# A depthwise convolution computed in long rows on VectorE, started one weight block sooner, with the mean pooling in a lane of its own

## The chip, the cores and the metric

The kernel runs on one core of a Trainium2 chip. The metric is device time in microseconds (us) of one execution of the whole program; of several executions the median is taken. The engines are TensorE (PE in the profile, with its weight loads as PEld), VectorE (DVE), ScalarE (ACT), GpSimd (POOL) and SyncE (SP), which issues nearly all the DMAs here.

## The reference, cut to what matters

The reference is one step of a two-layer diffusion backbone: 128 prompt tokens and 2048 latent tokens of width 1024. Each layer projects the tokens once, cuts the 3072 result columns among four mixers of width 256, concatenates what they give (each gated by a SiLU) and projects again. The change touches two of the mixers, the pooling and the convolution:

```python
def trunk_layer(x, cond, p, ctx=None):
    h = x * (1 + scale) + shift
    u = h @ p['w_in'] + p['b_in']
    (a_x, a_g, nq, nk, nv, n_g, c_v, c_glu, c_g, gq, gk, gv, g_g) = jnp.split(u, SPLIT_POINTS, axis=-1)
    a_out = pool_mix(a_x, p['pool_w'], p['pool_scale'])     # centred means over 2, 4, 8, 16 tokens, minus self
    c_out = conv_mix(c_v, c_glu, p['conv_w'], p['conv_b'], p['conv_ln_g'], p['conv_ln_b'], p['conv_pw'])
    ...                                                     # neighbourhood attention, grouped-query attention
    mixed = jnp.concatenate([a_out * jax.nn.silu(a_g), n_out * jax.nn.silu(n_g),
                             c_out * jax.nn.silu(c_g), g_out * jax.nn.silu(g_g)], axis=-1)
    x = layer_norm(DEEPNORM_ALPHA * x + gate * (mixed @ p['w_out'] + p['b_out']), p['ln_g'], p['ln_b'])

def conv_mix(val, glu, w_dw, b_dw, g, b, w_pw):
    z = val * jax.nn.sigmoid(glu)
    z = lax.conv_general_dilated(z, ...) + b_dw             # 31 taps along the tokens, each channel by itself
    z = jax.nn.silu(layer_norm(z, g, b))                    # over the 256 channels
    return z @ w_pw
```

## The kernel before, in words

Each layer has four phases: phase 1 is the input projection and all that can be done beside it, phase 2 the grouped-query attention, phase 3 the neighbourhood attention, phase 4 the output projection with its LayerNorm. Only phase 1 is touched.

Phase 1 walks the tokens in two halves: three chunks of 384 tokens, then chunks of 384, 384 and 256 (`CH`, `HALVES`). In each half it goes through the twelve entries of `BLOCKS`, 256 result columns each: `cx0` and `cx1` (value and gate of the convolution, 128 channels each), `cg` (its output gate), `gkv` and `gq` (keys, values and queries of the grouped-query attention), `ax` and `ag` (pooling input and gate), `nv`, `nk`, `nq`, `ng`, `gg`. Each product is made of three passes over pairs of a high and a low part, since PE's fast format keeps fewer bits: L306 to L308. `prep_w` loads the next block's weights in two pieces and splits each: ScalarE writes the high part `whi` (L430), POOL subtracts it to get `wlo` (L431). In the first half the split weights are also stored, in the second they are loaded back.

A projection tile goes to a PSUM bank of a pool of five (`ps_u`). Tiles of `gkv`, `gq` and `nv` have tokens on the partitions and are emptied by VectorE (`evac_tok`, for `nv` into the tile `nve`, which a DMA then stores); the others have channels there and are emptied by ScalarE (`evac_ch`). For `gkv` and `gq` a key norm follows: a square on ScalarE (`sq`, L665), a sum on VectorE (`rs`, L668), a product and a split on POOL (`ks`, L729), transposes on PE into `ps_d` (L735). `ps_d` is a second pool, of three banks, which all the side work shares.

After every projection tile `tick()` runs. It takes pending steps of `Later` and then advances the lanes, which are lists of generators; each `yield` ends a step. Lane A has the convolution pieces (`conv_job`), lane B what follows each (`conv_post`) and the pooling pieces (`pool_job`), lane C the max passes of the neighbourhood attention, lane D the modulation. A piece (`CONV_JOBS`) is the prompt with 128 tokens or 252 latent tokens in the first half, 208 in the second; there are five in a half. `conv_job` loads a piece with its margins into `cz`, for both channel blocks of 128. VectorE does 22 of the 31 taps as multiply-adds into `cacc` (the first as a product); ScalarE does the other nine, each as a product (L767) that POOL adds to a second sum (L768), and POOL joins both sums (L776). Two pieces may be open at once, and their taps alternate. `conv_post` transposes a piece on PE, normalises it (L800 to L811), transposes it back, applies SiLU, splits it and multiplies by the pointwise weights. `pool_job` forms the window sums by doubling (L855 to L863), subtracts and scales, splits, multiplies by the group weights and gates.

The order that each engine follows is not the order of this code: a scheduler places the instructions by a simulated timeline when the kernel is built, with the order of emission and the `issue_after` marks as bounds. Each engine then works strictly in its order.

Of the kernel before, what the change touches and what calls it, by code (L numbers as in the profile page):

```python
# [39 lines left out]
]  # L40
BLOCKS = [
# [79 lines left out]
class Kern:  # L121
# [314 lines left out]
    def split(self, pool, tag, src_ap, shape, load_engine=None):  # L436

        nc = self.nc
        w = self.b1.tile(shape, F32, tag="j32", name="spl")
# [7 lines left out]
    def _phase1(self, l):  # L447
        nc, A, S, v = self.nc, self.A, self.S, self.lv[l]
        self.later = Later()
        laneA, laneB, laneC, laneD = Lane(), Lane(), Lane(), Lane()  # L450
        self.conv_open = 0
        self.cg_done = -1
# [22 lines left out]
        NA, NB = (1,1), (1,2)  # L475

        def tick(ins):

            self.later.tick()
            last.append(getattr(ins, "ins", ins))  # L480
            with self.tc.issue_after(last[-2] if len(last) > 1 else last[-1]):
                for _ in range(NA[half]):
                    laneA.step()
                for _ in range(NB[half]):
                    laneB.step()
                laneC.step()
                if len(last) % 2:
                    laneC.step()
                laneD.step()
# [3 lines left out]
        for half in range(2):  # L493
            for b, (name, _) in enumerate(BLOCKS):
# [54 lines left out]
        while laneA.step() | laneB.step() | laneC.step() | laneD.step():  # L549
# [126 lines left out]
    def rms(self, l, name, t0, nt, nh, qb, rs):  # L676
# [22 lines left out]
        def s2(t):  # L699
# [15 lines left out]
            if name == "gq":  # L715
# [6 lines left out]
                if tg == 0:  # L722
                    qp = self.rp.tile([128, 4, 2, 64], F32R, tag="qp", name="qp", bufs=1)
# [20 lines left out]
    def conv_job(self, l, job, laneB):  # L744
        nc, S, v = self.nc, self.S, self.lv[l]
        prompt, a, b, sz = job
        n = b - a
        while self.conv_open == 2:
            yield
        self.conv_open += 1  # L750
        z = self.b2.tile([128, 2, 286], F32, tag="cz", name="cz")
        src = S["z_p"] if prompt else S["z_l"]
        nc.sync.dma_start(z[:, :, :n + 30], src[:, a:b + 30].rearrange("(c p) t -> p c t", p=128))
        acc = self.b2.tile([128, 2, 256], F32, tag="cacc", name="cacc")
        yield
        i = 0
        for c in range(2):
            ac2 = self.b1.tile([128, 256], F32, tag="cac2", name="cac2")
            cw = v["cw"]
            nc.scalar.activation(  # L760
                ac2[:, :n], z[:, c, 0:n], AF.Identity, bias=v["cvec"][:, 0, c:c + 1], scale=cw[:, c, 0:1]
            )
            nc.vector.tensor_scalar(acc[:, c, :n], z[:, c, 1:1 + n], cw[:, c, 1:2], None, op0=ALU.mult)
            for k in range(2, CW):
                if k % 7 in (0, 3):
                    tm = self.b2.tile([128, 256], F32, tag="jo", name="ctm")
                    nc.scalar.activation(tm[:, :n], z[:, c, k:k + n], AF.Copy, scale=cw[:, c, k:k + 1])  # L767
                    nc.gpsimd.tensor_tensor(ac2[:, :n], ac2[:, :n], tm[:, :n], op=ALU.add)  # L768
                else:
                    nc.vector.scalar_tensor_tensor(  # L770
                        acc[:, c, :n], z[:, c, k:k + n], cw[:, c, k:k + 1], acc[:, c, :n], op0=ALU.mult, op1=ALU.add
                    )
                i += 1
                if i % 8 == 0:
                    yield
            nc.gpsimd.tensor_tensor(acc[:, c, :n], acc[:, c, :n], ac2[:, :n], op=ALU.add)  # L776
# [929 lines left out]
```

## Time and profile before

| | us |
|---|---|
| three executions | 2950.91, 2958.63, 2963.24; median 2958.63 |
| the profiled execution: its time | 2961.56 |
| its span (first to last instruction) | 2959.8 |
| busy in it: PE | 2780.4 (94%) |
| VectorE | 2010.5 (68%) |
| POOL | 1339.0 (45%) |
| ScalarE | 1221.3 (41%) |

The whole profile is one execution. Rows of the view by windows give, for a stretch of time, each engine's busy time with its instructions, PE's granted clock (1.00 is 2.4 GHz, 0.50 is 1.2 GHz) and the share of DMA in use. The list of waits names an engine's tile and line, then what released it. A timeline is the instructions of one engine in order of time; "x45" there means 45 of them in one row, and the time beside it is their sum. Shares of busy time over a whole span say little here, since phase 1 and the attention phases have different limits.

### The profile page before, as it was taken

The page shows a single profiled execution, that of the slowest core. Times are in us where ns is not written, and L with a number is a line of the kernel's source. Part 1 is how long each engine was busy: PE and PEld are TensorE (multiplying, and loading weights), DVE is VectorE, ACT ScalarE, POOL GpSimd, SP SyncE. Part 2 cuts the span into 40 slices and gives each one's busy share as a digit, 9 for nine tenths or more (in the row PEclk, how much of TensorE's full clock was granted, in tenths as well). Part 3 has the DMA queues.
Part 4 walks back from the last instruction along what each step waited for, and adds up shares of the span by engine and source line. Part 5 has one row for each costly group of instructions (what it writes and reads, how often), then busy time and mean ns, then how long its engine had stood idle before and what let it go on. Part 6 is the DMA issues. An engine that isn't in the chain of part 4 may idle for free. (4 is left out here: it accounts for less than half of the span.)

```text
span 2959.8 us, 46887 instructions
## 1 busy us (share of the span) xinstructions
PE 2780.4 (94%) x16944; PEld 2285.5 (77%) x16944; DVE 2010.5 (68%) x4119; ACT 1221.3 (41%) x2278; POOL 1339.0 (45%) x1074
## 2 busy tenths in 40 slices
PE   7988999999899999999989789989999999999998
PEld 6878999889655556887779789988995555578887
DVE  2696157965578886749854881579655888776587
ACT  4454433543344445542223554335423444465211
POOL 3676323542466666014326674245424666730232
PEclk9999999999999999999999999999999999999999
DMA  9655586566271005646754556744654511066442
GB/s 304 213 182 179 184 249 201 169 202 175 66 170 32 25 20 151 162 137 229 234 171 136 168 171 185 218 147 148 208 152 94 131 34 29 15 184 181 133 167 104
DMA packets 387464, 448.32 MB, mean 151 GB/s; under 512 B 53920, under 2 KB 342688, under 8 KB 385440
## 3 DMA queue, kind: packets, MB, share of 16 engines
q1 hardware_dynamic: 387232, 445.32, 49.9%
q8 instruction: 134, 2.20, 0.3%
q14 instruction: 98, 0.80, 0.1%
HBM read 279.82 MB, written 165.39 MB: 150 GB/s over the span
## 5 line engine op out<-in xcount | busy, mean ns | idle before, releaser
L306 PE MATMUL ps_u<-hhi,whi 128*128 128x384 f32 (+1 forms) x1728 | 572.2, 334 | 6.7 <-ACT hhi L389 6.7
L307 PE MATMUL ps_u<-hlo,whi 128*128 128x384 f32 (+1 forms) x1728 | 573.2, 332 | 1.8 <-POOL hlo L391 1.3
L308 PE MATMUL ps_u<-hhi,wlo 128*128 128x384 f32 (+1 forms) x1728 | 571.9, 331 | 0.7 <-POOL wlo L431 0.7
L1038 POOL TENSOR_TENSOR zp<-zp,e 128x1024 f32<-128x1024 f32 x160 | 386.6, 2416 | 206.4 <-ACT e L1020 202.9
L1020 ACT ACTIVATE e<-ps_d 128x1024 f32<-128x1024 f32 x288 | 292.1, 1025 | 358.3 <-PE ps_d L1015 342.6
L770 DVE SCALAR_TENSOR_TENSOR cacc<-cz,small,cacc 128x208 f32<-128x208 f32 (+2 forms) x840 | 402.8, 536 | 0.3
L306 PEld LDWEIGHTS ps_u<-hhi,whi 128*128 128x128 f32 x1728 | 329.2, 191 | 14.8 <-ACT hhi L389 9.3
L307 PEld LDWEIGHTS ps_u<-hlo,whi 128*128 128x128 f32 x1728 | 330.1, 191 | 5.6 <-POOL hlo L391 2.0
L308 PEld LDWEIGHTS ps_u<-hhi,wlo 128*128 128x128 f32 x1728 | 329.9, 191 | 1.9 <-POOL wlo L431 1.1
L768 POOL TENSOR_TENSOR cac<-cac,ctm 128x208 f32<-128x208 f32 (+2 forms) x320 | 235.8, 737 | 148.9 <-ACT ctm L767 103.9
L946 DVE TENSOR_REDUCE mx<-ps_s 128x1 f32<-128x512 f32 (+1 forms) x374 | 228.5, 631 | 104.3 <-PE ps_s L943 99.8
L1478 POOL TENSOR_TENSOR mlo<-mx,mhi 128x512 fp32r<-128x512 f32 x66 | 109.4, 1677 | 418.9 <-ACT mhi L1474 418.9
L1026 PE MATMUL ps_a<-e,gvv 128*64 128x512 f32 x1152 | 278.2, 604 | 0.0
L306 PE MATMUL ps_u<-whi,hhi 128*128 128x256 f32 x816 | 240.7, 295 | 4.0 <-ACT ev L558 4.0
L307 PE MATMUL ps_u<-wlo,hhi 128*128 128x256 f32 x816 | 237.4, 291 | 0.3 <-POOL wlo L431 0.3
L308 PE MATMUL ps_u<-whi,hlo 128*128 128x256 f32 x816 | 237.4, 291 | 0.0
L767 ACT ACTIVATE ctm<-cz,small 128x208 f32<-128x208 f32 (+2 forms) x320 | 148.0, 473 | 157.3 <-POOL cac L768 101.0
L431 POOL TENSOR_TENSOR wlo<-ws,whi 128x512 fp32r<-128x512 f32 x92 | 150.1, 1642 | 132.9 <-ACT whi L430 121.1
L1508 PE MATMUL ps_d<-wol,mhi 128*128 128x512 f32 x512 | 200.5, 392 | 0.0
L1507 PE MATMUL ps_d<-woh,mhi 128*128 128x512 f32 x512 | 200.4, 391 | 0.0
L1509 PE MATMUL ps_d<-woh,mlo 128*128 128x512 f32 x512 | 200.3, 391 | 0.0
L1015 PE MATMUL ps_d<-q,k 65*128 65x512 f32 x576 | 185.0, 402 | 13.0 <-DMA k<-s_k 13.0
(269 smaller groups left out, 5742.6 us busy)
## 6 DMA issues: line engine op xcount, KB each, us to landing
ws<-in_w_in SPq DMA_DIRECT2D x80, 256.0 KB
mw<-in_w_mod SPq DMA_DIRECT2D x32, 512.0 KB
nq<-s_nq SPq DMA_DIRECT2D x64, 256.0 KB
mx<-s_mix SPq DMA_DIRECT2D x16, 1024.0 KB
s_gate<-ev SPq DMA_DIRECT2D x80, 192.0 KB
s_qh<-qT SPq DMA_DIRECT2D x34, 256.0 KB
x<-in_x SPq DMA_DIRECT2D x17, 512.0 KB
s_xT<-xo SPq DMA_DIRECT2D x17, 512.0 KB
```

The lines of the kernel that those rows point to most:

```text
L306: mm(p, ah, bh, start=(k == 0), stop=False)
L307: mm(p, ah, bl, start=False, stop=False)
L308: return mm(p, al, bh, start=False, stop=(k == 7))
L768: nc.gpsimd.tensor_tensor(ac2[:, :n], ac2[:, :n], tm[:, :n], op=ALU.add)
L770: nc.vector.scalar_tensor_tensor(acc[:, c, :n], z[:, c, k:k + n], cw[:, c, k:k + 1], acc[:, c, :n], op0=ALU.mult, op1=ALU.add)
L946: r = nc.vector.tensor_reduce(mx[:, h, i:i + 1], p[:, :n], axis=AX.X, op=ALU.max)
L1020: nc.scalar.activation(e, s, AF.Exp)
L1026: nc.tensor.matmul(acc[kv * 64:(kv + 1) * 64, :], vv[:, j, kv * 64:(kv + 1) * 64], e[:, kv * 512:(kv + 1) * 512], start=(j == 0), stop=(j ...
L1038: nc.gpsimd.tensor_tensor(zp, zp, e, op=ALU.add)
L1507: nc.tensor.matmul(o, hi[:, k, :], woh[:, k, ns], start=(k == 0), stop=False)
L1508: nc.tensor.matmul(o, hi[:, k, :], wol[:, k, ns], start=False, stop=False)
L1509: nc.tensor.matmul(o, lo[:, k, :], woh[:, k, ns], start=False, stop=(k == 7))
```

## The change

The convolution of a half is one job now, instead of five. For each channel block of 128 it loads the half's whole row (`CONV_LEAD` = 158 columns of prompt with margin and 1008 latent columns in the first half, 1040 columns in the second) into one buffer `cz`, and does all 31 taps on VectorE over that whole row, each adding into the same `cacc`. Channel block 0 begins after block `cx0`, channel block 1 after `cx1`; before, nothing began until `cx1` was done. When all rows are done the five pieces go to `conv_post`, as before, without three idle steps in it and with one buffer `s32` for each channel block.

The pooling has its own lane P and works on one channel block of one piece at a time, with its own buffers (`px`, `pg`, `phi`, `plo`) and the next load issued ahead. `tick` takes one step of lane A in `gkv` and `gq` and two elsewhere, two of lane B, and one or two in turn of lanes P and C. `nve` has one buffer where it had two, `qp` takes the tag of `qd`, and `split` the tag `czs`.

```diff
@@ _phase1
-        NA, NB = (1,1), (1,2)
...
             with self.tc.issue_after(last[-2] if len(last) > 1 else last[-1]):
-                for _ in range(NA[half]):
+                odd = len(last) % 2
+                for _ in range(1 if name in ("gkv", "gq") else 2):
                     laneA.step()
-                for _ in range(NB[half]):
+                for _ in range(2):
                     laneB.step()
-                laneC.step()
-                if len(last) % 2:
+                for _ in range(2 if odd else 1):
+                    laneP.step()
                     laneC.step()
                 laneD.step()
...
+                if name == "cx0":
+                    laneA.add(self.conv_job(l, half, laneB))
                 if name == "cx1":
-                    for job in CONV_JOBS[half]:
-                        laneA.add(self.conv_job(l, job, laneB))
+                    self.cx1_done = half
                 if name == "ag":
-                    for job in CONV_JOBS[half]:
-                        laneB.add(self.pool_job(l, job))
+                    laneP.add(self.pool_jobs(l, half))
@@ evac_tok
-            e = self.e2.tile([128, 256], F32, tag="nve", name="nve")
+            e = self.e2.tile([128, 256], F32, tag="nve", name="nve", bufs=1)
@@ conv_job
-        while self.conv_open == 2:
+        a, b = CONV_SPAN[half]
+        lead = CONV_LEAD if half == 0 else 0
+        n = lead + b - a
+        acc = self.b1.tile([128, 2, CONV_LEAD + 1008], F32, tag="cacc", name="cacc")
+        for c in range(2):
+            while c == 1 and self.cx1_done < half:
+                yield
+            cs = slice(c * 128, (c + 1) * 128)
+            z = self.b1.tile([128, CONV_LEAD + 1008 + CW - 1], F32, tag="cz", name="cz")
+            if lead:
+                nc.sync.dma_start(z[:, :lead], S["z_p"][cs, :])
+            nc.sync.dma_start(z[:, lead:n + CW - 1], S["z_l"][cs, a:b + CW - 1])
             yield
...
-            nc.vector.tensor_scalar(acc[:, c, :n], z[:, c, 1:1 + n], cw[:, c, 1:2], None, op0=ALU.mult)
-            for k in range(2, CW):
-                if k % 7 in (0, 3):
-                    tm = self.b2.tile([128, 256], F32, tag="jo", name="ctm")
-                    nc.scalar.activation(tm[:, :n], z[:, c, k:k + n], AF.Copy, scale=cw[:, c, k:k + 1])
-                    nc.gpsimd.tensor_tensor(ac2[:, :n], ac2[:, :n], tm[:, :n], op=ALU.add)
-                else:
-                    nc.vector.scalar_tensor_tensor(
-                        acc[:, c, :n], z[:, c, k:k + n], cw[:, c, k:k + 1], acc[:, c, :n], op0=ALU.mult, op1=ALU.add
-                    )
-                i += 1
-                if i % 8 == 0:
-                    yield
-            nc.gpsimd.tensor_tensor(acc[:, c, :n], acc[:, c, :n], ac2[:, :n], op=ALU.add)
-        laneB.add(self.conv_post(l, job, acc), soon=True)
+            for k in range(1, CW):
+                nc.vector.scalar_tensor_tensor(
+                    acc[:, c, :n], z[:, k:k + n], cw[:, c, k:k + 1], acc[:, c, :n], op0=ALU.mult, op1=ALU.add
+                )
+                yield
+        for i, job in enumerate(CONV_JOBS[half]):
+            o = 0 if job[0] else lead + job[1] - a
+            laneB.add(self.conv_post(l, job, acc[:, :, o:o + job[2] - job[1]]))
@@ pool_job -> pool_jobs
+        items = [(job, c) for job in CONV_JOBS[half] for c in range(2)]
+        nxt = load_x(*items[0])
         yield
+        for i, (job, c) in enumerate(items):
+            x = nxt
...
+            nc.scalar.activation(yhi[:, :n], y, AF.Copy)
+            nc.gpsimd.tensor_tensor(ylo[:, :n], y, f32(yhi[:, :n]), op=ALU.subtract)
+            if i + 1 < len(items):
+                nxt = load_x(*items[i + 1])
             yield
...
```

The three places below show the order on an engine, before and after. The first is VectorE in layer 0, first half, where the convolution starts. `cacc` rows are convolution taps, `ev` the gating of the convolution's input, `qb` and `gve` the emptying of `gkv`, `mo` the modulation. Before:

```order
L770 SCALAR_TENSOR_TENSOR cacc<-cz,small,cacc 128x128 x2
L576 SCALAR_TENSOR_TENSOR ev<-ev 128x384
L770 SCALAR_TENSOR_TENSOR cacc<-cz,small,cacc 128x252 x2
L770 SCALAR_TENSOR_TENSOR cacc<-cz,small,cacc 128x128 x2
L770 SCALAR_TENSOR_TENSOR cacc<-cz,small,cacc 128x252 x2
L770 SCALAR_TENSOR_TENSOR cacc<-cz,small,cacc 128x128 x2
```

And of the change:

```order
L577 SCALAR_TENSOR_TENSOR ev<-ev 128x384 x3
L763 TENSOR_SCALAR cacc<-cz,small 128x1166
L767 SCALAR_TENSOR_TENSOR cacc<-cz,small,cacc 128x1166 x2
L577 SCALAR_TENSOR_TENSOR ev<-ev 128x384
L767 SCALAR_TENSOR_TENSOR cacc<-cz,small,cacc 128x1166 x11
L359 TENSOR_TENSOR mo<-mo,ps_d 2x128
L767 SCALAR_TENSOR_TENSOR cacc<-cz,small,cacc 128x1166 x7
L655 TENSOR_TENSOR qb<-ps_u,btok 128x128
L658 TENSOR_TENSOR gve<-ps_u,btok 128x128
```

The alternating short taps of two pieces have become rows of 1166 columns that all add into one buffer.

The second place is POOL from the same point on: `wlo` is the weight split, `cac` and `cacc` the convolution's adds, `qb` and `ks` the key norm. Before:

```order
L431 TENSOR_TENSOR wlo<-ws,whi 128x512 x4
L768 TENSOR_TENSOR cac_940<-cac_940,ctm 128x128 x6
L431 TENSOR_TENSOR wlo<-ws,whi 128x512
L768 TENSOR_TENSOR cac_940<-cac_940,ctm 128x128 x2
L431 TENSOR_TENSOR wlo<-ws,whi 128x512 x3
L776 TENSOR_TENSOR cacc<-cacc,cac_940 128x128
```

And of the change:

```order
L433 TENSOR_TENSOR wlo<-ws,whi 128x512 x12
L694 TENSOR_TENSOR qb<-qb,qkn 128x128 x3
L730 TENSOR_TENSOR ks<-qb,ks 128x2x64 x3
L694 TENSOR_TENSOR qb<-qb,qkn 128x128 x3
L433 TENSOR_TENSOR wlo<-ws,whi 128x512 x2
```

The convolution's adds are gone from between the weight splits.

The third place is VectorE in block `nv` of layer 0's second half: `nve` empties a projection tile, `mx` is a max pass, `cst`, `cmv`, `crs` and `czs` the normalisation of a convolution piece, `jo` a gated output, `pA` and `pB` window sums of the pooling. Before:

```order
L644 TENSOR_TENSOR nve<-ps_u,btok 128x256
L946 TENSOR_REDUCE mx<-ps_d 128x1
L644 TENSOR_TENSOR nve<-ps_u,btok 128x256 x3
L800 BN_STATS cst<-ps_d 104x6 x2
L802 BN_AGGR cmv<-cst 104x2 x2
```

And of the change:

```order
L645 TENSOR_TENSOR nve<-ps_u,btok 128x256
L834 TENSOR_TENSOR jo<-ps_d,jg 128x208 x2
L899 SCALAR_TENSOR_TENSOR jo<-ps_d,small,pg 128x208
L952 TENSOR_REDUCE mx<-ps_d 128x1 x2
L863 TENSOR_TENSOR pA<-px 128x223
L645 TENSOR_TENSOR nve<-ps_u,btok 128x256
L866 TENSOR_TENSOR pB<-pA 64x221
```

Between two emptyings there is now work of three lanes, where there was that of one or two.

## Rows read from the trace of the kernel before

**Rows 1.** View by windows: A and B stretches, and two single blocks; columns first.

```profile
core 0: us, PE busy (x) PEld busy (x) DVE busy (x) ACT busy (x) POOL busy (x), PEclk, DMA share, GB/s
90.20:269.80 179.60, 154.53 (x1110) 145.31 (x1109) 144.67 (x348) 93.33 (x209) 131.76 (x139) 0.95 0.58 187
269.80:422.50 152.70, 145.93 (x1049) 141.23 (x1047) 53.79 (x136) 54.15 (x113) 51.19 (x51) 0.98 0.66 207
476.70:626.90 150.20, 141.23 (x1101) 131.97 (x1098) 135.53 (x375) 73.00 (x173) 74.65 (x101) 0.99 0.63 199
626.90:761.40 134.50, 131.81 (x889) 128.54 (x888) 62.20 (x140) 45.67 (x99) 40.40 (x57) 1.00 0.50 152
1555.50:1580.80 25.30, 25.30 (x146) 25.30 (x145) 10.20 (x26) 9.57 (x22) 9.55 (x12) 1.00 0.48 156
1580.80:1761.10 180.30, 149.25 (x966) 145.04 (x964) 133.10 (x325) 91.71 (x194) 130.06 (x131) 0.92 0.50 160
1761.10:1894.60 133.50, 132.77 (x853) 132.17 (x852) 50.87 (x123) 50.99 (x102) 51.22 (x52) 1.00 0.65 196
1923.20:1946.70 23.50, 23.50 (x154) 23.50 (x154) 11.17 (x29) 4.58 (x10) 1.41 (x2) 1.00 0.50 150
1946.70:2094.10 147.40, 133.44 (x936) 130.86 (x935) 131.55 (x352) 70.70 (x163) 77.87 (x101) 0.94 0.55 173
2094.10:2230.60 136.50, 133.35 (x889) 129.56 (x888) 68.89 (x161) 46.48 (x99) 40.47 (x57) 0.99 0.51 149
```

**Rows 2.** View by windows, VectorE's instructions that read `cz` alone, four A stretches.

```profile
90.20:269.80 179.60, 87.34 (x180) 0.95 0.58 187
476.70:626.90 150.20, 90.16 (x201) 0.99 0.63 199
1580.80:1761.10 180.30, 84.56 (x165) 0.92 0.50 160
1946.70:2094.10 147.40, 85.89 (x186) 0.94 0.55 173
```

**Rows 3.** Weight splits (ns min/median/max), then timelines of VectorE and POOL: start, us.

```profile
L431 POOL TENSOR_TENSOR wlo<-ws,whi x92: 1263/1297/14333, 48.8 to 1872.2; 128x512 fp32r<-128x512 f32 x92
1589.63 17.59 DVE L770 SCALAR_TENSOR_TENSOR cacc<-cz,small,cacc 128x252 f32<-128x252 f32 x45
1594.03 14.33 POOL L431 TENSOR_TENSOR wlo<-ws,whi 128x512 fp32r<-128x512 f32 x1 [3.18 <-ACT whi L430]
```

**Rows 4.** Waits from 1605 to 1652 us: us in total, times, longest us.

```profile
DVE rs L668 <- ACT sq L665: 23.8, 6, 16.5
ACT cac L760 <- POOL cacc L776: 15.3, 3, 14.4
PE ps_d L735 <- POOL ks L729: 9.0, 1, 9.0
```

**Rows 5.** Timeline of VectorE from 2846 us (phase 4): start, duration.

```profile
2846.28 1.21 DVE L1500 TENSOR_TENSOR y<-ps_d,gb 128x1024 f32<-128x1024 f32 x1
2847.53 1.23 DVE L1501 TENSOR_TENSOR y<-y,x 128x1024 f32<-128x1024 f32 x1
2850.35 1.28 DVE L1524 SCALAR_TENSOR_TENSOR y<-y,mv,lng 128x1024 f32<-128x1024 f32 x1
```

**Rows 6.** Timelines of POOL and VectorE from 1329 us (phase 4).

```profile
1329.21 3.52 POOL L1478 TENSOR_TENSOR mlo<-mx,mhi 128x512 fp32r<-128x512 f32 x2
1329.29 2.29 DVE L1493 SCALAR_TENSOR_TENSOR x<-x,gbo 128x1024 f32<-128x1024 f32 x1 [2.60 <-POOL gbo L1458]
1331.61 2.20 DVE L1501 TENSOR_TENSOR y<-y,x 128x1024 f32<-128x1024 f32 x1
```

**Rows 7.** View by windows, line L811 alone, first A stretch.

```profile
90.20:269.80 179.60, 3.16 (x5) 0.95 0.58 187
```

**Rows 8.** Timelines of SP's queue and of VectorE, a load and its reader.

```profile
403.05 0.39 SPq L851 DMA_DIRECT2D px<-s_axl  x1
412.16 0.44 DVE L860 TENSOR_TENSOR pA<-px 128x267 f32<-128x267 f32 x1 [3.12 <-DMA px<-s_axl]
```

More of the change, by code (lines that the diff above doesn't have):

```diff
@@ L40 @@
 ]
+CONV_SPAN = [(0, 1008), (1008, 2048)]
+CONV_LEAD = NPR + CW - 1
 BLOCKS = [
@@ L438, in split @@
         nc = self.nc
-        w = self.b1.tile(shape, F32, tag="j32", name="spl")
+        w = self.b1.tile(shape, F32, tag="czs", name="spl")
         nc.sync.dma_start(w, src_ap)
@@ L722, in s2 @@
                 if tg == 0:
-                    qp = self.rp.tile([128, 4, 2, 64], F32R, tag="qp", name="qp", bufs=1)
+                    qp = self.rp.tile([128, 4, 2, 64], F32R, tag="qd", name="qp")
                     nc.vector.tensor_copy(qp, f32(ql).unsqueeze(2).to_broadcast([128, 4, 2, 64]))
@@ L742, in rms, with conv_job @@
             self.later.add(1 + (t + 1) // 2, lambda t=t: s2(t))
[L744 removed]
+    def conv_job(self, l, half, laneB):
         nc, S, v = self.nc, self.S, self.lv[l]
[L746 to L777 removed]
@@ L793, in conv_post @@
         nc.sync.dma_start(gt[:, :, :n], S["gate"][512:768, g0:g0 + n].rearrange("(c p) t -> p c t", p=128))
-        for _ in range(3):
-            yield
         for i in range(nt):
@@ L804, in conv_post @@
                 yield
-        self.conv_open -= 1
         yield
@@ L814, in conv_post @@
         yield
-        s32 = self.b1.tile([128, 2, 256], F32, tag="j32", name="j32")
+        yield
         shi = self.b1.tile([128, 2, 256], F32R, tag="jhi", name="jhi")
@@ L818, in conv_post @@
         for c in range(2):
+            s32 = self.b1.tile([128, 256], F32, tag="j32", name="j32")
             pj = self.bank("d")
@@ L865, in pool_job @@
                 nc.vector.tensor_tensor(B1[:, 2:m - 1], A1[:, 1:m - 2], A1[:, 3:m], op=ALU.add)
-                yield
                 nc.vector.tensor_tensor(A1[:, 4:m - 3], B1[:, 2:m - 5], B1[:, 6:m - 1], op=ALU.add)
                 nc.vector.tensor_tensor(B1[h, 8:m - 7], A1[h, 4:m - 11], A1[h, 12:m - 3], op=ALU.add)
+            yield
+            tmp = self.b1.tile([128, 2, 8], F32, tag="ptmp", name="ptmp")
+            ends = [(e, t0 - a) for e, t0 in ((0, 0), (1, seq - 8)) if a <= t0 < b]
@@ L872, in pool_job @@
                 )
-                for e, t0 in ((0, 0), (1, seq - 8)):
-                    if a <= t0 < b:
-                        o = t0 - a
-                        tmp = self.b1.tile([128, 8], F32, tag="ptmp", name="ptmp")
-                        nc.vector.tensor_tensor(tmp[r, :], f[r, 8 + o:16 + o], self.pedge[r, c, e, :], op=ALU.mult)
-                        nc.vector.tensor_tensor(y[r, c, o:o + 8], tmp[r, :], x[r, c, 8 + o:16 + o], op=ALU.subtract)
-            yield
-        yhi = self.b1.tile([128, 2, 256], F32R, tag="jhi", name="jhi")
@@ L881, in pool_job @@
-        ylo = self.b1.tile([128, 2, 256], F32R, tag="jlo", name="jlo")
-        for c in range(2):
-            nc.scalar.activation(yhi[:, c, :n], y[:, c, :n], AF.Copy)
-            nc.gpsimd.tensor_tensor(ylo[:, c, :n], y[:, c, :n], f32(yhi[:, c, :n]), op=ALU.subtract)
-        yield
-        yield
-        for c in range(2):
+            for e, o in ends:
+                nc.vector.tensor_copy(x[:, 8 + o:16 + o], tmp[:, e, :])
+            y = x[:, 8:8 + n]
+            yhi = self.b1.tile([128, 256], F32R, tag="phi", name="phi")
@@ L888, in pool_job @@
+            ylo = self.b1.tile([128, 256], F32R, tag="plo", name="plo")
+            nc.scalar.activation(yhi[:, :n], y, AF.Copy)
+            nc.gpsimd.tensor_tensor(ylo[:, :n], y, f32(yhi[:, :n]), op=ALU.subtract)
+            if i + 1 < len(items):
+                nxt = load_x(*items[i + 1])
+            yield
+            yield
             pj = self.bank("d")
-            nc.tensor.matmul(pj[:, :n], self.plh[:, c, :], yhi[:, c, :n], start=True, stop=False)
-            nc.tensor.matmul(pj[:, :n], self.plh[:, c, :], ylo[:, c, :n], start=False, stop=False)
```

58 lines of the change are left out of this document (34 added, 24 removed).

## The prediction

> **What bounds the kernel now.** I read the busy shares first (PE 94% of the span), then the granted clock and busy time stretch by stretch, then PE's waits and what lay before them, and last the VectorE and POOL timelines. Only phase 1 is touched. For each layer and half I cut it into A (blocks cg, gkv, gq, ax, ag) and B (nv, nk, nq, ng, gg), at the first projection matmul of a block; [rows 1] gives these eight stretches.
>
> The floor is PE's. A block that nothing disturbs takes 25.3 us in the first half and 23.5 in the second, with PE busy throughout at clock 1.00, the full 2.4 GHz [rows 1]. That last one holds 10 other matmuls besides its 144. The price of such an "other" matmul (transposes, finishing products) comes from B of layer 1's first half: 133.5 us against 5 x 25.3 = 126.5, with 853 records of which 792 are projections, so 7.0 / 61 = 0.115 us each. A second-half block without them is then 23.5 - 1.1 = 22.4 us. PE's order holds 172 and 100 others in A of the first halves (layer 0, layer 1) and 199 and 117 in the second, so if nothing waited the four would need 146, 138, 135 and 126 us. They take 179.6, 180.3, 150.2 and 147.4 [rows 1]. So some 113 us are lost in A, and little in B.
>
> What is lost there is PE waiting on a coupled VectorE, ScalarE and POOL. VectorE is busy 144.7 of 179.6 us, and 87.3 of that is convolution [rows 1, 2]. The worst case can be read event by event: VectorE runs 45 convolution ops in one unbroken train, 17.6 us, 0.391 us apart; a POOL subtraction that splits weights, whose median is 1.30 us, starts inside the train and takes 14.33 us [rows 3]. POOL is in order, so its convolution add behind it is late; ScalarE's next convolution op waits 14.4 us for that add, the square for the key norm behind it on ScalarE is 16.5 us late to VectorE, and PE then stands 9.0 us for the split keys [rows 4]. The clock of that A stretch is 0.92 [rows 1]: part of it ran at the lower level, after PE had stood idle.
>
> **The change, part by part.** *Convolution off ScalarE and POOL.* 320 ScalarE products, 320 POOL adds and 40 joining adds go. All 31 taps are on VectorE now: 248 long rows (1166 columns in the first half, 1040 in the second) for 880 short ones. Nothing on ScalarE waits for POOL's convolution any more, so the chain of [rows 4] can't form.
>
> *What a long row costs.* Each row adds into the same accumulator as the one before it, and so waits for it. A dependent op starts 0.03 to 0.04 us after its forerunner ends: 2846.28 + 1.21, then 2847.53 [rows 5]. A multiply-add with a pointer scalar over 1024 columns takes 1.28 us [rows 5], so 1.31 per link. The slope is at most (1.28 - 0.391) / (1024 - 252) = 1.15 ns a column, hence 1.31 + 142 x 0.00115 = 1.47 us for 1166 columns and 1.33 for 1040. Lower bound: no gap and 1.04 ns (1.28 us less a start of 0.21, estimated): 1.42 and 1.30.
>
> *POOL against VectorE.* In the old train POOL stayed out. At a dependent boundary it gets in: the subtraction of 1329.21 takes its turn, the op of 1331.61 waits 0.03 us for its forerunner, and both VectorE ops stretch, to 2.29 and 2.20 us from the 1.23 of 2847.53 [rows 5, 6]. So one POOL op of 512 columns costs the VectorE chain up to 0.97 us. Averaged over all sizes the trace shows less: 172 convolution ops at 0.391 (132 of them) and an estimated 0.27 (40) make 62 us, and 87.3 with the 8 first taps (4 us) were busy, so 21 us over 139 POOL ops, 0.15 each [rows 1, 2]. In the order of the changed kernel A keeps 56 POOL ops in a first half (20 of them the weight splits) and about 33 in a second, where the split weights are reloaded. I take 0.97 for half of the 20 and 0.15 for the rest: 17 us; second half 33 x 0.15 = 5. Bounds: 56 x 0.15 = 8 and twice my value.
>
> The Trainium skill, SBUF — State Buffer, Who interferes with whom, says that a VectorE op with two SBUF inputs and a POOL op that reads SBUF exclude each other, and that the second to issue blocks until the first finishes. Under that rule the weight split would have waited for one op of 0.39 us, not 13 us; here the trace differs. The rule speaks against the change, as each block now lasts three times as long: an estimate by it is 56 x 1.0 = 56 us more POOL waiting per first half, which POOL, with 30 to 50 us of work left in 150, would still hide, so the sum would be the same.
>
> *A, summed.* VectorE's other work there is its busy time less the convolution [rows 1, 2], less about 9 us of finishing ops that move to B (an estimate: three times their largest member, 3.16 us, [rows 7]). By the order 62, 53, 54 and 54 of the long rows fall into A.
> - Layer 0, first half: 62 x 1.47 = 91, other 57.3 - 9 = 48, POOL 17: 156, and 5 for idle. PE needs 126.5 + 132 others x 0.115 = 142. So 161.
> - Layer 1, first half: 79 + 39.5 + 17 = 136 and 5; PE 133. So 141.
> - Layer 0, second half: 70.5 + 36 + 5 = 112; PE 112 + 134 x 0.115 = 127. So PE, 131 with some waits.
> - Layer 1, second half: 72 + 36.5 + 5 = 114; PE 118. So 122.
>
> That is 555 us for 657.5: -102.
>
> *B gets work.* Finishing (normalisation, pointwise product) and pooling of all five pieces of a half now follow in B, twelve steps each, two per tick, pooling in its own lane. By PE's order 243 more other matmuls stand in the four B stretches: x 0.115 = +28. The lag that nv carries in layer 0's first half (152.7 us, PE's need 126.5 + 157 x 0.115 = 144.6) mostly goes: -5. Chains with three PSUM banks between them will make PE wait a little; the second-half B of layer 1 shows 136.5 against 112 + 121 x 0.115 = 126, some 10 us over for three finished pieces and the wide max passes; for two pieces more I add 3.5 a half: +14. Bounds: 0 and +40.
>
> *At no cost.* The new `nve` single buffer, the merged `qp` tag, `czs` for the weight loads, the accumulator's single buffer: covered by PE running ahead over five banks, and by pieces being done before the next half's convolution starts; the first of these is priced as a rival.
>
> Sum: -102 + 28 - 5 + 14 = -65 us on the profiled execution of 2961.6: 2896. It lies 2.9 above the median of the runs, 2958.6, so about 2893; its span is 1.8 below its time.
>
> **Rivals.**
> 1. *Neither VectorE nor the chains ever bind.* Then A is PE's need, 142 + 133 + 127 + 118 = 520, -137; +28, -5: -114, 2845. For it: ScalarE and POOL are relieved. Against: in a first half VectorE is over PE's need even on the lower bounds (62 x 1.42 + 48 + 8 = 144).
> 2. *VectorE becomes the bound outright.* Twice the collisions in the first halves, 176 and 156, and 138 and 130 with waits behind rows of 1.4 us in the second: A 600, -57; +28 - 5 + 14: -20, 2939. For it: the token blocks gkv and gq are emptied by VectorE, now from behind long rows.
> 3. *Slower: the single `nve` buffer.* VectorE may not empty the next token tile of nv before the store of the last has landed, and max reductions, statistics and gated outputs wait behind it, with PE's three banks. PE delivers a tile about every 25.3 / 9 + 0.8 = 3.6 us. A transfer issued at 403.05 was waited for until 412.16, 8.7 us after its issue [rows 8]; with 0.42 for the op and 0.32 to issue that makes 9.4 us a tile, 5.8 too many, x 34 tiles = +197, less the 14 already counted: 3076. It decides from the point where it eats 79 us, 2.3 a tile, or a landing of 5.2 us; many transfers were quicker.
> 4. *POOL is starved by the long chain.* If dependence gives it no entry, the weight splits of gkv wait through the 18 rows in cg, 26 us, in both first halves, and PE behind them, partly at the lower clock: +26 to +52 and as much again in gkv: 2960 or so, no change. Against it: [rows 6]. This would also be the case in which the change doesn't loosen the coupling.
>
> **How the numbers follow.** Forecast 0.50, rival 1 0.15, rival 2 0.15, rival 3 0.12, rival 4 0.08. No change means within 0.5%, 15 us, about what a measurement of this kernel can tell. Forecast and rival 1 are faster but for 0.015; rival 2 sits on that edge, 0.09 faster and 0.06 same; rival 3 0.02 same and 0.10 slower; rival 4 0.02, 0.03, 0.03. That makes 0.75, 0.12, 0.13. The forecast's own range is 2870 to 2920. The range for 8 in 10 reaches down to rival 1 (2843) and up past rivals 2 and 4 to 2964; most of rival 3 stays outside.
>
> **What would show it.** Right: A of the first halves near 160 and 141 us with VectorE over 90% busy and PE's clock near 1; second halves at PE's pace; long rows 1.4 to 1.5 us apart, stretched by about 1 us where a weight split gets in; no POOL op beyond some 3 us in A; ScalarE never waiting for POOL there; B longer by 5 to 10 us each. Wrong: VectorE idle in A while PE waits (chains bind, not throughput); POOL ops of tens of us (rival 4); VectorE waiting for `s_nv` stores in nv (rival 3); or B longer by 20 us and more.

## The result and the profile after

The changed kernel takes 2887.55 us (median of 4 runs, 2885.37 to 2889.32) against 2959.32: a ratio of 0.9761, 95% interval 0.9739 to 0.9782. The forecast was 2893. Its profiled execution took 2889.32 us with a span of 2887.5, 72.3 shorter than before.

The view by windows, the same eight stretches as in [rows 1]: A, then B, of layer 0's first half and second half, then of layer 1's.

```profile
core 0: us, PE busy (x) PEld busy (x) DVE busy (x) ACT busy (x) POOL busy (x), PEclk, DMA share, GB/s
89.70:248.00 158.30, 147.59 (x1071) 139.20 (x1070) 151.90 (x239) 49.94 (x114) 75.77 (x57) 0.98 0.64 205
248.00:412.00 164.00, 155.34 (x1115) 147.03 (x1113) 53.67 (x136) 63.90 (x131) 51.62 (x53) 1.00 0.69 215
462.10:592.50 130.40, 129.59 (x1037) 122.81 (x1033) 111.58 (x206) 36.01 (x87) 39.13 (x33) 1.00 0.69 215
592.50:731.60 139.10, 137.24 (x946) 134.54 (x944) 62.04 (x155) 49.30 (x96) 25.03 (x33) 1.00 0.50 151
1543.90:1696.20 152.30, 139.23 (x927) 137.19 (x926) 141.85 (x222) 50.44 (x106) 67.32 (x57) 0.96 0.55 179
1696.20:1842.60 146.40, 142.69 (x920) 139.47 (x920) 52.36 (x123) 61.53 (x119) 50.49 (x52) 1.00 0.66 203
1892.90:2012.10 119.20, 118.14 (x871) 117.27 (x869) 112.25 (x196) 33.33 (x75) 36.00 (x33) 1.00 0.59 188
2012.10:2153.60 141.50, 137.40 (x946) 134.02 (x944) 62.80 (x157) 49.60 (x97) 24.82 (x33) 1.00 0.53 154
```

The four A stretches lost 97.3 us (560.2 for 657.5), the four B gained 33.8, the blocks `cx0` and `cx1` lost 7.7, all else 1.1. ScalarE's and POOL's busy time in A of the first halves has about halved (93 to 50, 132 to 76 us), VectorE's has grown. The same windows for the instructions that read `cz` answer to [rows 2]: VectorE spends more time on the convolution in a first half than before, less in a second.

```profile
89.70:248.00 158.30, 99.46 (x62) 0.98 0.64 205
462.10:592.50 130.40, 69.93 (x53) 1.00 0.69 215
1543.90:1696.20 152.30, 86.14 (x53) 0.96 0.55 179
1892.90:2012.10 119.20, 73.16 (x55) 1.00 0.59 188
```

The weight splits (ns: least, median, most), then VectorE and POOL in the place of [rows 3], answer to the shut-out there: the longest split is 2.64 us instead of 14.33. A row alone takes 1.42 us; beside a split it takes 2.26.

```profile
L433 POOL TENSOR_TENSOR wlo<-ws,whi x92: 1274/1308/2639, 49.5 to 1823.5; 128x512 fp32r<-128x512 f32 x92
```

```profile
1576.56 1.42 DVE L767 SCALAR_TENSOR_TENSOR cacc<-cz,small,cacc 128x1166 f32<-128x1166 f32 x1
1578.10 2.26 DVE L767 SCALAR_TENSOR_TENSOR cacc<-cz,small,cacc 128x1166 f32<-128x1166 f32 x1
```

```profile
1577.39 1.74 POOL L433 TENSOR_TENSOR wlo<-ws,whi 128x512 fp32r<-128x512 f32 x1 [3.85 <-ACT whi L432]
```

What PE waits for in layer 1's first A now, from the list of waits (us in total, times, longest): no longer 9 us at once as in [rows 4], but three times each for the split keys and for the high part of the queries, at most 3.9 us at once.

```profile
PEld ps_d L736 <- POOL ks L730: 7.6, 3, 3.9
PEld ps_d L736 <- ACT qd L718: 7.1, 3, 3.5
```

A sum over phase 1 of both layers makes the account shorter. PE's idle time is a stretch less PE's busy time. Before it is 104.8 us (79.1 of it in A), after 52.8 (25.7 in A). PE's busy time falls as well, from 1340.9 to 1321.6 us, though PE does the same matmuls (1506 besides the projections, before and after): fewer of them run at the lower clock. PE was busy at 0.50 for 72.3 us of phase 1 before and for 34.3 after; at the full clock these 38.0 us of work take half, which is the 19. The mean clock in the A stretches of the first halves went from 0.95 and 0.92 to 0.98 and 0.96. Idle 52.0, busy 19.3: that is the gain.

### The profile page after: what moved, and what is told of

The parts are those of the page before. It is cut to its first block, busy times and chain, and to the rows that moved or that the text cites. A ratio compares the mean times of both kernels' runs of the same rounds, so it can differ in the third digit from the quotient of the medians.

```text
span 2887.5 us, 45425 instructions
## 1 busy us (share of the span) xinstructions
PE 2761.1 (96%) x16944; PEld 2267.1 (79%) x16944; DVE 1964.9 (68%) x3503; ACT 1078.7 (37%) x1922; POOL 1099.2 (38%) x714
## 5 line engine op out<-in xcount | busy, mean ns | idle before, releaser
L767 DVE SCALAR_TENSOR_TENSOR cacc<-cz,small,cacc 128x1166 f32<-128x1166 f32 (+1 forms) x240 | 355.9, 1483 | 3.5
L433 POOL TENSOR_TENSOR wlo<-ws,whi 128x512 fp32r<-128x512 f32 x92 | 139.6, 1527 | 192.5 <-ACT whi L432 180.2
L1011 PE MATMUL ps_d<-q,k 128*128 128x512 f32 x576 | 186.0, 405 | 2.7 <-ACT e L1026 2.7
L1040 DVE TENSOR_TENSOR zd<-zd,e 128x1024 f32<-128x1024 f32 x80 | 139.6, 1746 | 47.2 <-ACT e L1026 47.2
```

The source lines that it names most:

```text
L767: nc.vector.scalar_tensor_tensor(acc[:, c, :n], z[:, k:k + n], cw[:, c, k:k + 1], acc[:, c, :n], op0=ALU.mult, op1=ALU.add)
L1011: nc.tensor.matmul(s[:, kv * 512:(kv + 1) * 512], k1[kv][:, j * 128:(j + 1) * 128], q1[:, 2 * kv:2 * kv + 2, :].rearrange("p h t -> p (h t ...
```

## The experiments

All ratios are to the kernel before, timed on the same chip beside each kernel. Phase 1's PE idle time, as above, is given for each. Every variant is placed anew by the scheduler, so a difference of a few us, of single blocks above all, can also come from another order.

| run | median us | ratio, 95% interval | PE busy / idle in phase 1 |
|---|---|---|---|
| before | 2959.32 | 1 | 1340.9 / 104.8 |
| the change | 2887.55 | 0.9761 (0.9739 to 0.9782) | 1321.6 / 52.8 |
| halves | 2896.88 | 0.9777 (0.9750 to 0.9805) | 1322.1 / 60.3 |
| pieces | 2931.5 | 0.9900 (0.9874 to 0.9926) | 1336.5 / 80.1 |
| b_alldve | 2889.26 | 0.9766 (0.9737 to 0.9795) | 1319.1 / 56.5 |
| fewer | 2888.96 | 0.9753 (0.9722 to 0.9783) | 1314.5 / 57.6 |
| nopool | 2897.25 | 0.9789 (0.9766 to 0.9813) | 1325.6 / 68.0 |
| noact | 2936.25 | 0.9922 (0.9906 to 0.9938) | 1337.9 / 88.8 |
| bufs | 2970.8 | 1.0034 (1.0008 to 1.0059) | 1340.9 / 105.3 |
| nveev | 2890.11 | 0.9764 (0.9736 to 0.9791) | 1325.4 / 53.4 |
| start | 2891.21 | 0.9767 (0.9741 to 0.9792) | 1317.2 / 52.3 |
| lag3 | 2887.45 | 0.9766 (0.9737 to 0.9795) | 1323.6 / 50.6 |
| spans | 2896.47 | 0.9798 (0.9771 to 0.9824) | 1326.0 / 57.7 |
| poolB | 2944.7 | 0.9943 (0.9924 to 0.9961) | 1314.2 / 49.4 |

**Is it that POOL gets in? (halves, pieces)**

```diff
+            cuts = ((0, n // 2), (n // 2, n))
             for k in range(1, CW):
+                for p, q in cuts:
+                    nc.vector.scalar_tensor_tensor(
+                        acc[:, c, p:q], z[:, k + p:k + q], cw[:, c, k:k + 1], acc[:, c, p:q], ...)
```

> Every long row is cut into two column halves (583 or 520 columns), issued one after the other, so that neighbours on VectorE no longer depend on each other; the work is the same. VectorE needs the same time for it: by the trace an independent neighbour of 252 columns starts 0.391 us after the last and a column costs 1.04 ns, so two halves take 2 x 0.736 = 1.47 us where a row of 1166 takes 1.45. Theory (POOL gets in only where VectorE waits for its own result, and this is what freed the A stretches): the weight splits on POOL are shut out again, some for 10 us and more, PE and ScalarE wait behind them, A of the first halves goes from 158 and 152 us back towards 170 to 180, the whole to 2915 to 2960 us. Rival (the gain is only that ScalarE and POOL have less to do): weight splits stay under 3 us, 2880 to 2895 us, since VectorE even loses the stretches of 0.85 us that a split costs it now.

Half of the theory held and half fell, and the time lies between the two ranges. The rows of VectorE and of POOL in layer 0's first half show that the shut-out can come back once neighbours are independent (the rows are also half as long):

```profile
97.50 12.60 DVE L770 SCALAR_TENSOR_TENSOR cacc<-cz,small,cacc 128x583 f32<-128x583 f32 x17
```

```profile
100.86 10.40 POOL L433 TENSOR_TENSOR wlo<-ws,whi 128x512 fp32r<-128x512 f32 x1 [6.11 <-ACT whi L432]
```

It is not the rule, though. A little later in the same stretch two splits get in between such rows at once, and the next row is stretched each time, to 1.82 us from 0.82:

```profile
110.23 13.99 DVE L770 SCALAR_TENSOR_TENSOR cacc<-cz,small,cacc 128x583 f32<-128x583 f32 x15
```

```profile
114.58 1.38 POOL L433 TENSOR_TENSOR wlo<-ws,whi 128x512 fp32r<-128x512 f32 x1 [3.32 <-ACT whi L432]
116.16 1.55 POOL L433 TENSOR_TENSOR wlo<-ws,whi 128x512 fp32r<-128x512 f32 x1 [0.20 <-ACT whi L432]
```

Of the 13 splits of this run that begin between two independent rows, 3 took over 3 us and 10 under 2 us; of the 12 that begin between dependent rows in the changed kernel, none took over 2.42. What decides whether an independent train lets a split in is not shown. Halves start 0.737 us apart, as estimated. But the kernel is at most slightly slower: 9 us between the medians, with intervals that overlap, and PE idles 7.5 us more. A late weight split alone does little harm.

```diff
+            cuts = [(j * n // 5, (j + 1) * n // 5) for j in range(5)]
+            for p, q in cuts:
+                for k in range(1, CW):
+                    nc.vector.scalar_tensor_tensor(acc[:, c, p:q], z[:, k + p:k + q], ...)
```

> The row is cut into five column pieces of about 233 (second half 208) columns, and each piece runs through its 31 taps before the next begins: five times as many instructions, each dependent on the one before it. A dependent op of 233 columns takes 0.45 + 0.03 us by the trace of before, so a tap over the whole row takes 2.4 us instead of 1.45, in the second half 2.25 instead of 1.33. Theory (VectorE's throughput bounds A, and dependence alone lets POOL in, however short the rows): A of the first halves gets 62 and 53 times 0.95 us more work, some 50 us each, of the second halves 50 us each of which PE hides a part; some of it slides into B; 2990 to 3060 us; POOL's weight splits stay under 4 us. Rival 1 (POOL gets in because the rows are long, so that there are few issues): weight splits of 10 us and more. Rival 2 (VectorE has slack): 2890 to 2910 us.

Neither number came, and the premise failed: the scheduler dealt the five pieces out tap by tap, so that neighbours were independent again, 0.37 us apart (39 rows in 14.60 us), and a weight split took 11.12 us. The run says nothing on short dependent rows, then. It does say that five times the instructions cost 44 us against the change, with 27 us more PE idle time, 15 of it in B.

**One part alone (b_alldve)**

```diff
-                if k % 7 in (0, 3):
+                if False:
```

(and the first tap on VectorE, no join; in the kernel before)

> The kernel before, with all 31 taps on VectorE and no product on ScalarE or add on POOL for them, pieces, order and lanes otherwise as before (short rows, two pieces alternating). This is the one part of the change that takes work off ScalarE and POOL, alone. VectorE's convolution in A grows by 9/22, 87 to 123 us, and its total in a first half from 145 to some 180. Theory: without the long dependent rows this part alone gains nothing, because POOL's splits and key norms are still shut out by the alternating pieces and VectorE has more to do: 2950 to 3010 us, weight splits up to 10 us and more. Rival (relief of ScalarE and POOL is what pays): 2900 to 2930 us.

The theory falls, and the rival is outdone: this one part alone gives as much as the whole change, without long rows, an earlier start or new lanes. Its four A stretches by windows:

```profile
87.90:246.90 159.00, 150.01 (x1109) 142.00 (x1109) 155.68 (x418) 59.23 (x129) 83.94 (x60) 0.99 0.66 212
451.80:590.10 138.30, 135.17 (x1083) 128.02 (x1080) 130.22 (x405) 46.77 (x107) 40.41 (x38) 1.00 0.67 210
1538.00:1700.80 162.80, 143.62 (x963) 140.70 (x962) 149.77 (x395) 62.29 (x124) 83.06 (x60) 0.96 0.54 177
1889.30:2019.30 130.00, 124.49 (x919) 123.25 (x918) 127.42 (x381) 43.49 (x97) 27.49 (x38) 0.99 0.59 185
```

VectorE is as good as full in the first of them (155.68 of 159.00), and one split on POOL is shut out longer than ever. Here are 63 short rows on VectorE, and two weight splits on POOL, the first of which alone takes 21.12 us:

```profile
1548.85 21.40 DVE L768 SCALAR_TENSOR_TENSOR cacc<-cz,small,cacc 128x128 f32<-128x128 f32 x63
```

```profile
1550.26 22.36 POOL L431 TENSOR_TENSOR wlo<-ws,whi 128x512 fp32r<-128x512 f32 x2 [3.31 <-ACT whi L430]
```

**Does VectorE's throughput set A? (fewer)**

```diff
+                if half or k < CW - 6:
                     nc.vector.scalar_tensor_tensor(
```

> The changed kernel without the last six taps of each channel block in the first half of each layer (part of the convolution is left out), 12 rows of 1166 columns fewer in each first A. Theory (VectorE's throughput bounds A of the first halves, PE that of the second): A of layer 0's first half falls from 158 to about 145 us, of layer 1's from 152 to about 138, second halves stay; 2855 to 2865 us. Rival (what binds there is the chain from the emptying of a token tile over ScalarE and POOL to PE, not VectorE's throughput): 2880 us or more.

It doesn't. The windows show VectorE 22 us less busy in either first A (129.57 for 151.90, 119.83 for 141.85), and the stretches only 2.6 and 2.9 us shorter:

```profile
87.70:243.40 155.70, 145.78 (x1070) 137.83 (x1069) 129.57 (x226) 50.72 (x113) 72.09 (x57) 0.99 0.65 207
1546.30:1695.70 149.40, 136.75 (x925) 134.32 (x924) 119.83 (x211) 50.99 (x106) 67.61 (x57) 0.97 0.55 182
```

**Which engine's relief? (nopool, noact, bufs)**

```diff
-                    nc.gpsimd.tensor_tensor(ac2[:, :n], ac2[:, :n], tm[:, :n], op=ALU.add)
...
-            nc.gpsimd.tensor_tensor(acc[:, c, :n], acc[:, c, :n], ac2[:, :n], op=ALU.add)
```

> The kernel before without POOL's adds of the convolution (320 adds and 40 joins; ScalarE still makes its nine products a piece, nobody adds them, so nine of 31 taps are left out); VectorE keeps its 22 taps in short alternating rows. Since moving the taps off both engines gave the whole gain, the question is which of the two matters, or their coupling. Theory (ScalarE's products wait for POOL's starved adds to free their two buffers, and the key norm and the evictions wait behind them on ScalarE): nothing on ScalarE waits for POOL's adds, the whole gain and a little more, since VectorE has less to do than with 31 taps: 2870 to 2895 us, phase 1's PE idle time near 50 us. Rival 1 (POOL's own load makes the key norm and the splits late): the same, 2870 to 2895. Rival 2 (ScalarE's load): 2930 to 2950 us.

```diff
-                    nc.scalar.activation(tm[:, :n], z[:, c, k:k + n], AF.Copy, scale=cw[:, c, k:k + 1])
-                    nc.gpsimd.tensor_tensor(ac2[:, :n], ac2[:, :n], tm[:, :n], op=ALU.add)
+                    nc.gpsimd.tensor_tensor(ac2[:, :n], z[:, c, 0:n] if k == 3 else ac2[:, :n], z[:, c, k:k + n], op=ALU.add)
```

> The kernel before without ScalarE's products of the convolution; POOL adds the same number of rows, taken directly from the input tile (so nine of 31 taps lack their factor), and joins both sums as before. POOL has the same load and is as starved by VectorE's alternating rows, but ScalarE never waits for it there. Theory (the coupling through ScalarE costs the time): most of the gain, 2890 to 2915 us; weight splits of 10 us and more stay in the trace without harm. Rival 1 (POOL's own in-order queue, late for key norms, weight splits and low parts, costs the time): little gain, 2935 to 2960 us. Rival 2 (ScalarE's load): as the theory.

```diff
-                    tm = self.b2.tile([128, 256], F32, tag="jo", name="ctm")
+                    tm = self.b2.tile([128, 256], F32, tag="ctm", name="ctm", bufs=3)
-            ac2 = self.b1.tile([128, 256], F32, tag="cac2", name="cac2")
+            ac2 = self.b1.tile([128, 256], F32, tag="cac2", name="cac2", bufs=2)
```

> The kernel before with three buffers of their own for ScalarE's products (before: two, shared with the gated outputs) and two buffers for POOL's sum (before: one); no work is taken away. Theory (coupling of ScalarE to POOL through few buffers): ScalarE's waits for POOL's adds, 29.1 + 11.4 us in A of layer 0's first half, fall by a third to a half, and the time by 10 to 30 us, to 2930 to 2950 us. Rival 1 (POOL's own queue): no change, 2950 to 2960 us.

Of ScalarE's nine taps eight are products that POOL adds, 320 in all, and the first one starts POOL's sum (L760). Without POOL's adds most of the gain is there, and PE's idle time falls by 36.8 us; the time lies 2 us above the range that the theory and rival 1 shared. Without ScalarE's products, with POOL's adds kept, a third is there, and it falls by 16.0: rival 1's range. That third takes in both what ScalarE lost by waiting for late adds, as in [rows 4], and its own load. In layer 0's first A of the kernel before these were its waits for POOL:

```profile
ACT ctm L767 <- POOL cac L768: 29.1, 31, 5.8
ACT cac L760 <- POOL cacc L776: 11.4, 2, 11.1
```

So the larger part comes with the adds themselves. How an add on POOL makes PE wait can be followed in the longest wait of `noact`, 13.3 us for split keys, in layer 1's first half. The high part of a weight split is ready at 1594.92. POOL, first held by the split before it, then does joins and adds of the convolution from 1596.53 on, and gets to that split at 1611.31. Only then is the buffer of the weights free, and SP issues the next load into it. ScalarE waits 13.22 us for this load, and the square of the key norm stands behind it (rows of three timelines, by time):

```profile
1594.29 0.63 ACT L430 ACTIVATE whi<-ws 128x512 fp32r<-128x512 f32 x1 [3.40 <-PE ps_u L307]
1597.54 3.53 POOL L763 TENSOR_TENSOR cac<-cac,cz 128x128 f32<-128x128 f32 x7
1602.36 5.19 POOL L763 TENSOR_TENSOR cac<-cac,cz 128x252 f32<-128x252 f32 x7
1611.31 1.26 POOL L431 TENSOR_TENSOR wlo<-ws,whi 128x512 fp32r<-128x512 f32 x1
1612.60 0.38 SPq L424 DMA_DIRECT2D ws<-in_w_in  x1
1615.55 0.63 ACT L430 ACTIVATE whi<-ws 128x512 fp32r<-128x512 f32 x1 [13.22 <-DMA ws<-in_w_in]
1616.09 0.29 ACT L665 ACTIVATE sq<-qb 128x128 f32<-128x128 f32 x1
```

How much of the whole goes by this path is not shown. By the lists of waits of the four A stretches PE waited for split keys (`ks`) as long without the adds as with them, 15.8 us for 15.9. What fell are its waits for the finishing of the convolution (low part, join and gated output, 21.0 to 5.6) and for ScalarE's `qd` and `ctm` (12.0 to 0).

More buffers between the two bought nothing and perhaps lost 0.3%; neither range has that time. They shortened ScalarE's waits for the adds only from 40.5 to 34.9 us in the first of the stretches, and from 114.4 to 103.3 in all four. So the coupling was not taken away by this run, and what it costs is not read from it.

**The rest of the change, undone or varied (nveev, start, lag3, spans, poolB)**

```diff
-            e = self.e2.tile([128, 256], F32, tag="nve", name="nve", bufs=1)
+            e = self.b4.tile([128, 384], F32, tag="ev", name="nve")[:, :256]
```

> The changed kernel with the token tiles of nv emptied into the three eviction buffers that ScalarE's tiles use, instead of the single buffer of its own. In the trace of the changed kernel VectorE sat idle for 31.9 us in 16 waits for the stores of that buffer. Theory (that idle time of VectorE stands beside PE's work; the single buffer costs little): 2880 to 2890 us, nv of layer 0's first half from 38.6 to no less than 36 us. Rival (the single buffer holds PE's banks up and is why nv takes 5 us longer than its neighbours): 2865 to 2875 us.

Block `nv` of layer 0's first half did get shorter, 33.8 us for 38.6, which the theory had not allowed; the time as a whole didn't change. The buffer need not be the reason: with the single buffer kept, the same block took 30.4 us in `start` and 36.2 in `lag3`. PE's idle time in the `cx` blocks rose from 8.8 to 14.5 us.

```diff
-                if name == "cx0":
-                    laneA.add(self.conv_job(l, half, laneB))
                 if name == "cx1":
                     self.cx1_done = half
+                    laneA.add(self.conv_job(l, half, laneB))
```

> The changed kernel with the convolution of channel block 0 begun only after block cx1, as before (one part undone). Nine or ten of the rows of an A stretch are then done one block later. Theory (VectorE's throughput does not set A, as the run with fewer taps showed): 2885 to 2900 us, the finishing of the pieces starts later and B's idle time of PE, 18.3 us over the four, grows by 5 to 15. Rival (the head start is worth a block's rows, 10 x 1.4 us in each of four stretches): 2920 us and more.

The head start is worth nothing that can be measured: the theory's range. B's idle time of PE grew by 2.3 us only, to 20.6.

```diff
-                self.later.add(2, lambda: s3(...))
+                self.later.add(3, lambda: s3(...))
```

> The changed kernel with the transposes of the normed keys and queries issued three projection tiles after their split instead of two. In its A stretches PE is idle for 25.7 us, and the waits listed there are those transposes' for POOL's low part (14.7 us) and ScalarE's high part (12.1 us). Theory (what is left in A is the length of that chain, VectorE, ScalarE, POOL, PE, against the lag given to it): PE's idle time in A falls to 15 us or less, the whole to 2870 to 2882 us. Rival (the buffers of those tiles are taken for longer and the wait moves in front of the split): 2884 to 2895 us.

No gain: PE's idle time in A is 23.7 us instead of 25.7, and PE still waits as long for `ks`. What holds those last 25 us stays open.

```diff
+        for part in (jobs[:3], jobs[3:]):
...
+            acc = self.b1.tile([128, 2, 664], F32, tag="cacc", name="cacc", bufs=2)
...
+            for job in part:
+                laneB.add(self.conv_post(l, job, acc[:, :, o:o + job[2] - job[1]]))
```

> The changed kernel with the convolution of a half in two spans (662 and 504, in the second half 624 and 416 columns) instead of one: both channel blocks of the first span are done and handed to the finishing steps while the second span is still in work; two accumulators of 664 columns. By the trace a tap costs 0.91 + 0.75 us instead of 1.45, 14 us more on VectorE in a first A. Theory (VectorE has slack of that size, and what the change pays in B is that all five pieces come to their finishing at once): idle time of PE in B back from 18 us to 10 or less, 2872 to 2886 us. Rival (VectorE's extra time counts, or finishing in A disturbs the key norm there): 2895 to 2910 us.

The rival's range: the finishing moved into A as planned (A 599.6 us for 560.2, B 565.5 for 591.0), but B's idle time stayed at 19.2 us and that of A rose to 31.8.

```diff
-                    laneP.add(self.pool_jobs(l, half))
+                    laneB.add(self.pool_jobs(l, half))
```

> The changed kernel with the pooling appended to lane B, behind the finishing of the convolution, as before (the lane of its own undone; its own buffers and the one channel block at a time stay). Its ten steps of a half then come after the five pieces, late in B and into the next half's first blocks. Theory (the rest of the change only moves PE's work between stretches; none of it is worth more than some 10 us): 2883 to 2900 us, with A shorter by a few us and cx longer. Rival (the lane of its own is what keeps B from growing further): 2905 us and more.

This is the large miss. Phase 1 is even 10.8 us shorter (busy and idle, 1363.6 for 1374.4), but the time from layer 0's last projection tile to layer 1's first grows from 761.6 to 796.0 us, and from layer 1's last tile to the end from 733.9 to 769.4. The windows after layer 0's last tile show why, first without the lane and then, for comparison, in the change:

```profile
724.00:734.00 10.00, 1.30 (x5) 0.69 (x4) 2.51 (x6) 1.36 (x4) 4.56 (x3) 0.67 0.93 227
734.00:744.00 10.00, 1.30 (x3) 0.79 (x3) 2.84 (x7) 0.38 (x1) 0.62 (x1) 0.50 0.48 134
744.00:754.00 10.00, 2.55 (x6) 1.58 (x6) 4.48 (x11) 0.75 (x2) 1.25 (x2) 0.50 0.20 54
754.00:764.00 10.00, 1.34 (x4) 0.79 (x3) 5.71 (x20) 0.38 (x1) 0.62 (x1) 0.50 0.24 66
```

```profile
731.60:741.60 10.00, 2.98 (x8) 1.49 (x7) 0.00 (x0) 3.39 (x5) 3.97 (x2) 0.76 0.90 220
741.60:751.60 10.00, 10.00 (x33) 6.33 (x32) 6.55 (x11) 3.08 (x4) 4.75 (x2) 0.72 0.50 120
```

Six pooling steps, each with a load, a VectorE chain, a ScalarE copy and a POOL subtraction, run one after the other with nothing else for PE to do, at the lower clock. PE waits for each, 33.2 us in all for their high parts; the longest wait in its timeline:

```profile
741.54 0.54 PE L895 MATMUL ps_d<-phi,plh 128*128 128x208 f32 x1 [12.09 <-ACT phi L888]
742.24 0.54 PE L896 MATMUL ps_d<-plo,plh 128*128 128x208 f32 x1 [0.16 <-POOL plo L889]
742.58 0.42 PE L897 MATMUL ps_d<-phi,pll 128*128 128x208 f32 x1
```

No run was faster than the change or `b_alldve` beyond its interval. Of the kernels with all taps on VectorE all but `pieces` end between 49 and 61 us of PE idle time in phase 1, the change among them.

## Why the prediction came out right, and where it was not

- *The total and its two large terms held*: A was to lose 102 and lost 97.3; B was to gain 37 and gained 33.8. PE's busy time in B grew by 28.6 us for 28 predicted, its idle time there by 5.0 for 14 less 5. Within A two errors partly cancel: the first halves lost 49.3 us for 58, the second 48.0 for 45. The `cx` blocks' 7.7 us were not in the sum, and the 5 us of lag in `nv` did not go (38.6 us for 38.1).
- *The long rows* were sized right: 1.468 us apart where nothing else runs, for 1.47, and 1.337 for 1.33. A split stretches a row by 0.84 us, for 0.97; POOL's work in all, put at 17 us on the rows of a first half, added some 12 (60 rows took 98.1 us, and 52 took 85.3, at 1.42 alone). That POOL stays out of the old train was read from one split of 14.33 us; the median beside it, 1.30, says that most got in.
- *Second halves at PE's pace*: 130.4 and 119.2 for 131 and 122, PE busy 129.6 and 118.1. Right, and for the reason given.
- *First halves bound by VectorE*: the step that failed. 158.3 for 161 is near, 152.3 for 141 is not, and the reason is wrong in both, since 22 us less work on VectorE gave under 3; that 161 came near is luck. PE's need, some 6 us more of it than 142 and 133 (the lower clock accounts for about 3 and 6 of that, by the mean clocks of 0.98 and 0.96), and 11 and 13 us of waiting make the two stretches. In layer 1 VectorE's other work was 55.7 us (141.85 less 86.14), not 39.5: the pooling's first piece had moved in, and the key norm's small operations took longer. The prediction's sign of being right, VectorE over 90% busy there, came true (96 and 93%) and is still no proof that VectorE sets the stretch.
- *Convolution off ScalarE and POOL*: named first in the prediction, as the end of the chain in [rows 4], and alone it gives the whole gain. But the sum did not price it by itself, and the mechanism named, ScalarE behind a late add, is the smaller part: 23 us of 72 come when ScalarE is out of it and the adds stay. The larger comes with the adds on POOL itself; one wait shows how they can reach PE, what each path is worth stays open.
- *POOL let in by dependence* (rival 4 turned round): no split between dependent rows was shut out, but most between independent ones aren't either, and it is worth 9 us between the medians, which is not clear of the noise. The rule of the Trainium skill weighed in the prediction (SBUF — State Buffer, Who interferes with whom) was left without effect on the sum, and the time bears that out. `halves` shows both: one split waits through some 14 rows, not for one as by the rule, and others in the same stretch get in at once.
- *The lane of its own*: not priced by itself; it stands in the 42 us of work and waits for finishing and pooling in B. The run without it shows what the prediction never asked, namely what a late pooling would cost behind the last tile: 57 us. The parts beyond the first one thus cancel: finishing everything after the convolution would expose the pooling, and the lane hides it again.
- *Rivals*: 1 had PE's need in A near (520 us, for 534.5 busy) but no waits, and 25.7 came; 2 needed the VectorE bound; 3 saw its sign, 31.9 us of VectorE waiting for the stores in nv, but they cost nothing that shows, as the run with three buffers shows no change.

## What to carry to other kernels

Work handed to an idle engine is not free when that engine's in-order queue also carries short steps of a chain that a busy engine waits for: taking 320 small adds and 40 joins off POOL was worth 62 us, though POOL had 27 to 50% of its time free in the stretches concerned. An engine that fills a stretch need not set it; take some of its work away and look before sizing a change by it. And ask of each moved step where its last instance lands: a chain that ends behind the last projection tile costs its full latency.

## What the runs showed of the hardware

A weight split on POOL, 1.30 us alone, that begins while VectorE runs rows that don't depend on each other can be shut out for many of them: 10.40 us beside some 14 rows of 583 columns (`halves`), 21.12 us beside 59 rows of 128 (`b_alldve`). Most such splits get in, 10 of 13 in `halves` within 2 us. Between dependent rows all 12 got in within 2.42 us. One split of 512 columns that got in lengthened the VectorE row beside it from 1.42 to 2.26 us. PE, once it had stood idle behind phase 1 in `poolB`, was granted 0.50 of its clock for the few matmuls from 734 to 764 us.
